# Two fused transformer blocks on one core: the mixers' turns held to a distance in TensorE's queue, and some weight splits queued behind a branch

## The chip, the cores and the metric

The kernel runs on one core of a Trainium2 chip. The metric is the device time of one execution in microseconds (us), taken as the median of several runs. Besides the runs there is one profiled execution, whose trace gives the rows below. Of the core's engines TensorE (PE) does the matmuls and its weight loads (PEld), VectorE (DVE), ScalarE (ACT) and GpSimd (POOL) do the rest, and SyncE (SP) issues most of the transfers (DMA).

## The reference

A sequence of T = 512 tokens with D = 1024 features goes through two blocks, all in fp32.

```python
# first block, two layers
for l in range(2):
    p = h @ w_in[l]                       # 1024 -> the columns of four mixers
    ya = hgrn2(pa); yb = gla(pb)          # chunked gated linear attention, chunks of 64
    yc, v_first = rwkv7(pc)               # a recurrence over the tokens, 4 heads of 64
    yd = retnet(pd)                       # chunked retention
    h = layer_norm(a * h + concat(ya, yb, yc, yd) @ w_out[l])
    f = swiglu(h) if l == 0 else moe(h)   # 2816 hidden; or 8 experts of 1408, top 2
    h = layer_norm(a * h + f)
# second block
x = x + 0.5 * rms_norm(swiglu(rms_norm(x)))                  # ffn1, 2816 hidden
x = x + rms_norm(hybrid_mixer(rms_norm(x)))                  # RG-LRU and window attention
x = x + 0.5 * rms_norm(swiglu(rms_norm(x)))                  # ffn2
```

## The kernel before

**Matmuls and weights.** Activations lie with features on the 128 partitions and the 512 tokens along the free axis. An fp32 product is made from two reduced-precision halves of each side: a value is split into hi (a copy by ScalarE, L353) and lo (a subtraction by VectorE, L354), and a block of 128 x 128 weights costs three matmuls of 512 columns: hi x hi, hi x lo, lo x hi (`mm3`, L384 to L386; in `head_steps`, which begins a stage, L444, L445 and L447). Weights are split on the chip. A `Stream` (from L643) loads them in units of eight blocks (512 KB, on SyncE's queue, into a ring of raw tiles) and cuts each unit into four pieces of 256 columns (`piece`, L673), a split each; the halves lie in a ring of ten slots, `whi` and `wlo`, and a slot is free once TensorE has used it.

**The order of the work.** The program is written as one sequence. A scheduler then gives each engine its own queue: an instruction is put there when it is ready by the scheduler's reckoning, so an engine's queue can differ from the order in the code. Two means bind it: `keep_in_program_order` pins an instruction to its place among the pinned ones, and `tc.issue_after(i)` makes what is issued inside it stand behind instruction i in the queue of i's engine (an order of issue alone, with no wait for its end).

**The weave.** The mixers of the first block (`mixer1`, L1520, once for each layer) are written as generators that yield now and then with a cost; the code between two yields is called a turn here. `weave` (L795) draws turns from three streams, always from the one whose virtual time is lowest, and adds the turn's cost over the stream's weight. The first stream is the RWKV-7 recurrence in two pairs of heads (`rwkv_pair`, L1025), with many matmuls of 16 or 32 columns on 32 x 32 or 64 x 32 tiles (L1106, L1153); the second is the projections, the `gemm` turns: long runs of 512-column matmuls into a bank of `bkA` (L384 to L386), or 256-column ones (L871 to L873); the third is HGRN2, GLA and retention (`hg`, L1326, small matmuls at L1373; `ret`, L1470). The norms of heads in the scans go through `head_rstd` (L919): a matmul (L925), a copy on ScalarE, a transpose (L929), two VectorE instructions, a root on ScalarE (L937, with a load of its function table), and four transposes back (L940), all in one turn. The hybrid mixer of the second block uses the same `weave` with five streams (L2271).

**The branch.** In the second layer the experts run one after another. Near the end of the last one stands a branch (`tc.If`, L1961) for experts that got more tokens than fit; every engine passes it, and in the trace no instruction of the overflow code runs. Ahead of it the last expert's outputs are scaled into `last` (L1981 on ScalarE, L1982 on VectorE), and the scheduler has put splits of the first pieces of the next stage's weights (`f1gu`, the second block's ffn1, L2250 and on) there as well. Behind it `combine` (L2001) adds the experts' rows to the residual: for each of eight half tiles a few matmuls (L2011, L2020, L2022), an add on VectorE (L2024) and a square on ScalarE (L2025), both pinned. Then TensorE runs ten matmuls that compute nothing needed (`warm`, L328), transposes the rows (L1988), and ffn1 starts at L444.

Of the kernel before, what the change touches and what calls it, by code (L numbers as in the profile page):

```python
# [2 lines left out]

# [1 line left out]

# [7 lines left out]
AF = mybir.ActivationFunctionType  # L13
OP = mybir.AluOpType
# [628 lines left out]
class Stream:  # L643


    def __init__(self, K_, src, pool=None, bufs=None, own=0):
        self.K, self.src, self.u, self.j, self.ahead, self.ready = K_, src, -1, 8, [], []
        self.pool, self.bufs, self.own, self.units = pool, bufs, own, 0

    def fetch(self):  # L650
        self.ahead.append(self.load())
# [21 lines left out]
    def piece(self, raw):  # L673
        k = self.K
        if self.pool and self.units > self.own:
            t = self.pool.tile([P, 2, WC], F32R, name="wx", tag="wx", bufs=self.bufs)
            hi, lo = t[:, 0], t[:, 1]
        else:
            hi = k.ws.tile([P, WC], F32R, name="whi", tag="whi", bufs=WB)
            lo = k.ws.tile([P, WC], F32R, name="wlo", tag="wlo", bufs=WB)  # L680
        k.split(raw, hi, lo)
        return hi, lo

    def block(self):
# [49 lines left out]
WEAVEA = (1.0, 1.4, 1.8)  # L734
WEAVEB = (1.0, 1.3, 1.8)
NH32 = 4
WARM = 10
AHEAD = 1
STEP, LAG, LEAD = 4, 12, 4
RINGD, RINGO = 10, 8  # L740
LAG1, LEAD1, LAG2 = 12, 2, 18
# [50 lines left out]
        return self.pool.tile(shape, dt, name=name, tag=self.tag, bufs=self.bufs)  # L792


def weave(streams, weights):  # L795


    at = [0.0] * len(streams)
    live = set(range(len(streams)))
    now = 0.0  # L800
    while live:
        for n in sorted(live, key=lambda i: at[i]):
            try:
                c = next(streams[n])
            except StopIteration:
                live.remove(n)
                break
            if c is not None:
                now = at[n]
                at[n] += c / weights[n]  # L810
                break
            at[n] = max(at[n], now)
# [707 lines left out]
def mixer1(k, l, begin):  # L1520
    tc = k.tc
    with tc.tile_pool(name="mxc", bufs=1, reuse_waits="tile") as cp, \
            tc.tile_pool(name="mxa", bufs=1, reuse_waits="tile") as ap, \
            tc.tile_pool(name="mxb", bufs=1, reuse_waits="tile") as bp:
        sl = Slots(ap, "a", NA)
        st = k.stream(f"win{l}")
        if begin:
            k.load_x(sl, st)
        m = Mix(k, l, st, cp, ap, bp)
        if begin:  # L1530
            trig(k, sl)

        def chain(*gens):
            for g in gens:
                yield from g

        weave([chain(m.rwkv_pair(0), m.rwkv_pair(1)),
               chain(m.rwkv_in((6, 2, 0, 4, 5)), m.hg_in(0), m.rwkv_in((7, 8, 3, 1)), m.hg_gate(0), m.hg_in(1),
                     m.hg_gate(1), m.ret_in()),
               chain(m.hg(0), m.hg(1), m.ret())], (WEAVEA, WEAVEB)[l])  # L1540
        sT = []
        for f in range(0, KT, 2):
            t = m.a2(("ZR", "MB")[f // 4], [P, 2, T])
            sT += [t[:, 0], t[:, 1]]
        st = k.ln_stats(sl, 1 if l else 2)[l:]
        ws = k.stream(f"wout{l}", *(() if l else (Slots(bp, "b", NB), 0, KT - 2)))
        tot = Totals(*st)
        ys = (lambda q: m.yH[q]), (lambda q: m.yL[q])
        ro = k.moe if l else None
        if ro:  # L1550
            flat = lambda t: t.rearrange("p a b c -> p (a b c)")
            ro.open(sl, *[Cut(flat(m.a2("ZL", [P, NT, 2, P]))) for _ in range(2)])
        for f in range(KT):
            k.resid_in(f, sT)
            if f >= st[0].last and not l:
                continue
            ps = k.gemm_fm(ws, ys, KT, tot.first if f == KT - 1 else None)
            k.resid_out(f, ps, sT, st)
            if ro:
                ro.logits(f, sT[f])  # L1560
        if ro:
            ro.route(sT, tot, ap, m.yH[0])
        else:
            k.ln_end(ws, ys, KT, 2 * KT, sT, k.par(f"ln1g{l}"), k.par(f"ln1b{l}"), sl, st)
        if "y" in k.dbgs:
            for f in range(KT):
                t = sl.tile([P, T])
                k.nc.vector.tensor_tensor(t, m.yH[f].bitcast(F32), m.yL[f].bitcast(F32), op=OP.add)
                k.nc.sync.dma_start(k.dbgs["y"][f], t)
# [26 lines left out]
class Moe:  # L1596
# [404 lines left out]
    def combine(self, cp, acc):  # L2001

        k, nc = self.k, self.k.nc
        V, mm, pin = nc.vector, nc.tensor.matmul, self.k.tc.keep_in_program_order
        st = [k.sm.tile([P, 8], F32, name="cst") for _ in range(NT)]
        half = lambda i, n: acc[:, i, n * 512:(n + 1) * 512]

        banks = {}
        def first(i, n):
            b = banks[i, n] = k.bankA() if n else k.bankB()  # L2010
            return mm(b, cp[:, 1, 1, 0, i * P:(i + 1) * P], cp[:, 0, n, 0], start=True, stop=False)  # L2011

        def add(i):
            sl = slice(i * P, (i + 1) * P)
            for n in range(2):
                if n:
                    first(i, n)
                b = banks[i, n]
                rs = slice(64 * n, 64 * n + 64)
                mm(b, cp[:, 1, 1, 0, sl], cp[:, 0, n, 1], start=False, stop=False)  # L2020
                for q in range(2):
                    mm(b, cp[rs, 1, 1, 1, sl], cp[rs, 1, 0, q], start=False, stop=q == 1)  # L2022
                a = half(i, n)
                pin(V.scalar_tensor_tensor(a, b, 1.0, a, op0=OP.mult, op1=OP.add, accum_out=st[i][:, n:n + 1]))  # L2024
                pin(nc.scalar.activation(b, a, AF.Square, accum_out=st[i][:, 2 + n:3 + n]))  # L2025

        def var(i):
            s = [st[i][:, c:c + 1] for c in range(8)]
            pin(V.tensor_scalar(s[4], s[0], s[1], 1.0 / D, op0=OP.add, op1=OP.mult))
            pin(V.tensor_scalar(s[5], s[2], s[3], 1.0 / D, op0=OP.add, op1=OP.mult))  # L2030
            pin(V.scalar_tensor_tensor(s[5], s[4], s[4], s[5], op0=OP.mult, op1=OP.subtract))
            pin(nc.scalar.activation(s[6], s[5], AF.Sqrt, bias=k.eps[1e-5], scale=-1.0))

        def norm(i):
            s = [st[i][:, c:c + 1] for c in range(8)]
            pin(V.reciprocal(s[6], s[6]))
            pin(V.tensor_scalar(s[7], s[4], s[6], -1.0, op0=OP.mult, op1=OP.mult))

        def scale(i):
            s = [st[i][:, c:c + 1] for c in range(8)]  # L2040
            if i == 0:
                pin(nc.gpsimd.tensor_scalar(acc[:, i], acc[:, i], s[6], s[7], op0=OP.mult, op1=OP.add))
            elif i == 1:
                pin(nc.scalar.activation(acc[:, i], acc[:, i], AF.Identity, bias=s[7], scale=s[6]))
            else:
                pin(nc.scalar.activation(half(i, 0), half(i, 0), AF.Identity, bias=s[7], scale=s[6]))
                pin(V.tensor_scalar(half(i, 1), half(i, 1), s[6], s[7], op0=OP.mult, op1=OP.add))

        for i in range(NT):
            first(i, 0)  # L2050

        nc.scalar.activation(k.sm.tile([P, 1], F32, name="root"), cp[:, 0, 1, 1, :1].bitcast(F32), AF.Sqrt, bias=k.eps[1e-5], scale=0.0)
        for i in range(NT + 2):
            if i < NT:
                add(i)
            if i == NT - 1:
                k.warm(cp[:, 1, 1, 0], WARMC, k.bankA)
            if i >= 2:
                norm(i - 2)
            if 1 <= i <= NT:  # L2060
                var(i - 1)
            if i >= 2:
                scale(i - 2)
# [105 lines left out]
class Second:  # L2169
# [73 lines left out]
    def ffn(self, n, post, nxt):  # L2243
        k, nc, tc = self.k, self.k.nc, self.k.tc
        V = nc.vector
        with tc.tile_pool(name="ffn", bufs=1) as p, tc.tile_pool(name="ffnt", bufs=2) as p2:
            hH = p.tile([P, NH, T], F32R, name="hH")
            hL = p.tile([P, NH, T], F32R, name="hL")
            Rs = self.scale_rows(p2)
            st = k.stream(f"f{n}gu")  # L2250
            xs = k.xs()
            ps = finish(k.head_steps(st, xs, 0 if n == 1 else LEAD))
            ps += [k.gemm_fm(st, xs, KT, bank=k.bankB) for _ in range(AHEAD)]
# [12 lines left out]
    def mixer(self):  # L2266
        k, tc = self.k, self.k.tc
        with tc.tile_pool(name="m2y", bufs=1) as big:
            with tc.tile_pool(name="m2", bufs=1, reuse_waits="tile") as pool:
                m = Hybrid(k, self, big, pool)  # L2270
                weave([m.project(), m.lru(), m.heads(0), m.heads(1), m.attend()], WEAVE2)  # L2271
            with tc.tile_pool(name="m2o", bufs=1) as p:
                ws = k.stream("wo2", p, RINGO, KT - 2)
                self.post(ws, ((lambda a: m.yH[a]), (lambda a: m.yL[a])), KT, 2, 2 * KT, "mpost", 1.0, "pre2", p, LEAD)
# [289 lines left out]
```

## Time and profile before

| | us |
|---|---|
| median of 3 runs | 2657.43 |
| lowest and highest | 2655.86 and 2659.28 |
| the profiled execution | 2657.86 |
| its span in the trace | 2656.1 |
| TensorE busy | 2590.3 (98%) |
| VectorE busy | 1628.9 (61%) |
| ScalarE busy | 1344.3 (51%) |
| mean granted clock of TensorE | 0.988 |

The span is what the trace covers; the execution's own time is 1.8 us more. Busy is the time in which an engine has an instruction under way. An idle time is put down to what ended it: an engine with a tile and a line, a DMA, or "issue", which means that the engine waited for nothing that the profile shows. Matmuls overlap, so a matmul's duration is longer than its distance to the next; a line with x and a number joins that many alike. The granted clock is TensorE's as a share of full speed; it has two levels, 1.2 and 2.4 GHz. "ACTq" and "DVEq" are an engine's sequencer, not its work.

### The profile page before, as it was taken

To read this page: it belongs to the slowest core of one execution; us is meant where nothing else is said; L and a number is where in the kernel's file an instruction comes from. 1 tells how busy PE (TensorE), PEld (TensorE's weight loads), DVE (VectorE), ACT (ScalarE), POOL (GpSimd) and SP (SyncE) were. 2 spreads that over 40 slices of the span, in tenths; PEclk is the share of its full clock that TensorE was granted. 3 is DMA by queue.
4 is the path that set the end of the run, shared out by engine and by line. 5 is a ranking of instruction groups with operands and counts; after the bars stand their busy time and mean duration, and the time that the engine had idled before them with its cause. 6 is when DMAs were issued, how large, how long until landed. Compare 5 with 4: busy or idle time off the path is not lost. (4 is left out here: it accounts for less than half of the span.)

```text
span 2656.1 us, 48326 instructions
## 1 busy us (share of the span) xinstructions
PE 2590.3 (98%) x18669; PEld 2115.0 (80%) x18669; DVE 1628.9 (61%) x3383; ACT 1344.3 (51%) x2789; POOL 308.6 (12%) x391
## 2 busy tenths in 40 slices
PE   8999999999999999999999999999999999999998
PEld 6777688888877676798888888688888877888887
DVE  6655565444466555467888888665553578655533
ACT  5465344333343554366666666554433467444432
POOL 1101120000030010042233233100000100100000
PEclk9999999999999999999999999899999999999999
DMA  4111413223321112279887878523222212132222
GB/s 161 46 53 50 158 66 110 95 96 97 110 81 43 56 50 72 73 231 340 276 274 265 283 278 262 179 81 101 96 96 95 90 56 87 65 102 97 95 96 72
DMA packets 96330, 334.39 MB, mean 126 GB/s; under 512 B 12079, under 2 KB 15631, under 8 KB 96096
## 3 DMA queue, kind: packets, MB, share of 16 engines
q1 hardware_dynamic: 87520, 305.61, 34.3%
q0 software_dynamic: 8000, 24.95, 3.0%
q8 instruction: 149, 2.44, 0.4%
q10 hardware_dynamic: 576, 0.69, 0.1%
q14 instruction: 85, 0.70, 0.1%
HBM read 313.76 MB, written 17.45 MB: 125 GB/s over the span
## 5 line engine op out<-in xcount | busy, mean ns | idle before, releaser
L353 ACT ACTIVATE whi<-wraw 128x256 fp32r<-128x256 f32 x1172 | 475.9, 415 | 773.9 <-PE bkA L385 712.2
L354 DVE TENSOR_TENSOR wlo<-wraw,whi 128x256 fp32r<-128x256 f32 x1172 | 486.7, 423 | 582.6 <-ACT whi L353 563.2
L384 PE MATMUL bkA<-xH,whi 128*128 128x512 f32 x1352 | 537.2, 397 | 2.1 <-DVE sh L964 1.8
L385 PE MATMUL bkA<-xL,whi 128*128 128x512 f32 x1352 | 535.8, 396 | 0.0
L386 PE MATMUL bkA<-xH,wlo 128*128 128x512 f32 x1352 | 531.7, 393 | 0.0
L1921 PE MATMUL bkA<-xe,mhi 128*128 128x320 f32 x1392 | 358.3, 344 | 3.0 <-POOL xe L1782 1.6
L384 PEld LDWEIGHTS bkA<-xH,whi 128*128 128x128 f32 x1352 | 254.2, 188 | 68.7 <-issue 13.6
L385 PEld LDWEIGHTS bkA<-xL,whi 128*128 128x128 f32 x1352 | 254.6, 188 | 58.3 <-issue 9.6
L386 PEld LDWEIGHTS bkA<-xH,wlo 128*128 128x128 f32 x1352 | 254.2, 188 | 58.6 <-issue 7.0
L1923 PE MATMUL bkA<-xe,mlo 128*128 128x160 f32 x1218 | 287.7, 236 | 1.2 <-DVE mlo L354 1.2
L1921 PEld LDWEIGHTS bkA<-xe,mhi 128*128 128x128 f32 x1392 | 250.1, 189 | 4.3 <-POOL xe L1782 2.4
L1923 PEld LDWEIGHTS bkA<-xe,mlo 128*128 128x128 f32 x1218 | 233.1, 191 | 1.8 <-DVE mlo L354 1.7
L384 PE MATMUL bkA<-hH,whi 128*128 128x512 f32 (+1 forms) x548 | 204.2, 373 | 0.0
L385 PE MATMUL bkA<-hL,whi 128*128 128x512 f32 (+1 forms) x548 | 203.9, 372 | 0.0
L386 PE MATMUL bkA<-hH,wlo 128*128 128x512 f32 (+1 forms) x548 | 203.7, 372 | 0.0
L354 DVE TENSOR_TENSOR mlo<-mraw,mhi 128x1024 fp32r<-128x1024 f32 x105 | 139.9, 1334 | 36.8 <-ACT mhi L353 33.9
L353 ACT ACTIVATE mhi<-mraw 128x1024 fp32r<-128x1024 f32 x105 | 110.4, 1054 | 24.4 <-PE bkA L2096 11.1
L354 DVE TENSOR_TENSOR mlo<-wraw,mhi 128x1024 fp32r<-128x1024 f32 x79 | 104.6, 1327 | 23.1 <-ACT mhi L353 21.5
L385 PEld LDWEIGHTS bkA<-hL,whi 128*128 128x128 f32 x548 | 103.2, 188 | 18.1
L384 PEld LDWEIGHTS bkA<-hH,whi 128*128 128x128 f32 x548 | 103.2, 188 | 17.9
L386 PEld LDWEIGHTS bkA<-hH,wlo 128*128 128x128 f32 x548 | 103.1, 188 | 17.8
L354 DVE TENSOR_TENSOR mlo<-mlow,mhi 128x1024 fp32r<-128x1024 f32 x78 | 105.8, 1358 | 18.5 <-ACT mhi L353 15.9
(738 smaller groups left out, 4424.2 us busy)
## 6 DMA issues: line engine op xcount, KB each, us to landing
mraw<-moew SPq DMA_DIRECT2D x105, 512.0 KB
wraw<-moew SPq DMA_DIRECT2D x81, 512.0 KB
mlow<-moew SPq DMA_DIRECT2D x78, 512.0 KB
wraw<-win SPq DMA_DIRECT2D x76, 512.0 KB
wraw<-f0gu SPq DMA_DIRECT2D x44, 512.0 KB
wraw<-f1gu SPq DMA_DIRECT2D x44, 512.0 KB
wraw<-f2gu SPq DMA_DIRECT2D x44, 512.0 KB
wraw<-f0d SPq DMA_DIRECT2D x22, 512.0 KB
```

The lines of the kernel that those rows point to most:

```text
L353: nc.scalar.activation(hi, x, AF.Copy)
L354: nc.vector.tensor_tensor(lo, x, hi.bitcast(F32), op=OP.subtract)
L384: mm(ps, wH, xH, start=first, stop=False)
L385: mm(ps, wH, xL, start=False, stop=False)
L386: mm(ps, wL, xH, start=False, stop=last)
L1921: mm(ps, wH, xf[:, q], start=q == 0, stop=last, skip_group_check=True)
L1923: mm(ps[:, :C], wL, xe[:, q, 0], start=False, stop=False, skip_group_check=True)
```

## The change

`weave` gets the tile context and a distance, `behind`. It notes the last TensorE instruction of each turn that has any, and issues each turn inside `tc.issue_after` of the one noted `behind` turns ago. `mixer1` passes `BEHIND = 12`; the hybrid mixer passes a number that is never reached. The second part: `combine` notes its first add and its first square in `k.hold`; ffn1's stream takes this as `st.hold`, and the splits of its first two units (eight pieces) are issued inside `tc.issue_after` of these two. Both are orders of issue; no instruction is added, and none leaves.

```diff
 class Stream:
     def __init__(self, K_, src, pool=None, bufs=None, own=0):
-        self.pool, self.bufs, self.own, self.units = pool, bufs, own, 0
+        self.pool, self.bufs, self.own, self.units, self.hold = pool, bufs, own, 0, None
...
     def piece(self, raw):
...
-        k.split(raw, hi, lo)
+        with ExitStack() as order:
+            if self.hold and self.units <= 2:
+                for i in self.hold:
+                    order.enter_context(k.tc.issue_after(i.ins))
+            k.split(raw, hi, lo)
         return hi, lo
...
+BEHIND = 12
...
-def weave(streams, weights):
+def weave(tc, streams, weights, behind):
+    traced = tc.nc.cur_bb.bb.instructions
+    ends = []
+
+    def turn(s):
+        n = len(traced)
+        with tc.issue_after(ends[-behind]) if len(ends) >= behind else nullcontext():
+            c = next(s)
+        new = [i for i in traced[n:] if i.engine == mybir.EngineType.PE]
+        if new:
+            ends.append(new[-1])
+        return c
...
-                c = next(streams[n])
+                c = turn(streams[n])
...
 def mixer1(k, l, begin):
...
-        weave([chain(m.rwkv_pair(0), m.rwkv_pair(1)),
+        weave(tc, [chain(m.rwkv_pair(0), m.rwkv_pair(1)),
...
-               chain(m.hg(0), m.hg(1), m.ret())], (WEAVEA, WEAVEB)[l])
+               chain(m.hg(0), m.hg(1), m.ret())], (WEAVEA, WEAVEB)[l], BEHIND)
...
     def combine(self, cp, acc):
...
+        k.hold = None
...
-                pin(V.scalar_tensor_tensor(a, b, 1.0, a, op0=OP.mult, op1=OP.add, accum_out=st[i][:, n:n + 1]))
-                pin(nc.scalar.activation(b, a, AF.Square, accum_out=st[i][:, 2 + n:3 + n]))
+                done = (pin(V.scalar_tensor_tensor(a, b, 1.0, a, op0=OP.mult, op1=OP.add, accum_out=st[i][:, n:n + 1])),
+                        pin(nc.scalar.activation(b, a, AF.Square, accum_out=st[i][:, 2 + n:3 + n])))
+                k.hold = k.hold or done
...
     def ffn(self, n, post, nxt):
...
             st = k.stream(f"f{n}gu")
+            if n == 1:
+                st.hold = k.hold
...
     def mixer(self):
...
-                weave([m.project(), m.lru(), m.heads(0), m.heads(1), m.attend()], WEAVE2)
+                weave(tc, [m.project(), m.lru(), m.heads(0), m.heads(1), m.attend()], WEAVE2, 10 ** 6)
```

## Rows read from the trace of the kernel before

**Rows 1.** The page's part 1: busy us (share of the span) and instructions.

```profile
PE 2590.3 (98%) x18669; PEld 2115.0 (80%) x18669; DVE 1628.9 (61%) x3383; ACT 1344.3 (51%) x2789; POOL 308.6 (12%) x391
```

**Rows 2.** Table by stage: window, us, busy by engine, PEclk, DMA share, GB/s.

```profile
7.00:337.00 330.00, 319.17 (x4046) 235.33 (x4047) 196.72 (x494) 173.37 (x346) 29.77 (x53) 0.98 0.27 90
...
745.00:1082.00 337.00, 321.79 (x4108) 237.21 (x4109) 204.15 (x504) 170.48 (x342) 43.43 (x66) 0.98 0.19 62
...
1703.00:1735.00 32.00, 29.29 (x88) 16.80 (x89) 16.78 (x49) 17.08 (x36) 1.20 (x1) 0.68 0.06 18
```

**Rows 3.** TensorE's waits, 30:330: line, what ended them, us, times, longest us.

```profile
PE bkB L1373 <- issue: 2.6, 2, 1.9
PE bkB L1153 <- issue: 2.5, 3, 1.8
...
PE bkB L1106 <- issue: 0.5, 1, 0.5
```

**Rows 4.** TensorE's waits, 770 to 1010 us.

```profile
PE bkB L1153 <- issue: 5.0, 3, 2.1
PE bkB L1373 <- DVE Qp L1348: 1.4, 1, 1.4
...
PE bkA L871 <- issue: 0.8, 1, 0.8
PE bkB L1106 <- issue: 0.8, 1, 0.8
```

**Rows 5.** Table by stretches of 10 us, columns as in rows 2.

```profile
60.00:70.00 10.00, 9.83 (x274) 7.64 (x275) 2.64 (x7) 3.32 (x7) 0.00 (x0) 0.83 0.05 7
190.00:200.00 10.00, 9.45 (x227) 8.75 (x227) 4.56 (x10) 6.56 (x8) 0.00 (x0) 0.66 0.01 3
```

**Rows 6.** TensorE's timeline from 56 us: start, us, line, tiles, count, [idle before].

```profile
60.17 0.44 PE L1153 MATMUL bkB<-XT,Y 32*32 32x16 f32 x33 [1.75 <-issue]
...
61.25 0.78 PE L384 MATMUL bkA<-xH,whi 128*128 128x512 f32 x1
```

**Rows 7.** Timeline of TensorE, from 40 us.

```profile
46.21 0.39 PE L384 MATMUL bkA<-xH,whi 128*128 128x512 f32 x1
46.55 0.66 PE L940 MATMUL bkB<-ca,kk 128*128 128x128 f32 x4
```

**Rows 8.** Timelines of ScalarE, VectorE and TensorE at the branch.

```profile
1700.78 1.34 ACT L353 ACTIVATE whi<-wraw 128x256 fp32r<-128x256 f32 x4 [2.29 <-DMA wraw<-f1gu]
...
1703.39 0.41 DVE L354 TENSOR_TENSOR wlo<-wraw,whi 128x256 fp32r<-128x256 f32 x1
1703.72 0.74 DVE L1982 SCALAR_TENSOR_TENSOR last<-bkA,gs,last 128x512 fp32r<-128x512 f32 x1
1704.39 0.41 DVE L354 TENSOR_TENSOR wlo<-wraw,whi 128x256 fp32r<-128x256 f32 x1
...
1703.97 0.50 PE L2011 MATMUL bkB<-last 128*128 128x512 f32 x1 [1.41 <-ACTq L1961]
1705.19 1.08 PE L2011 MATMUL bkB<-last 128*128 128x512 f32 x3 [0.71 <-DVEq L1961]
```

**Rows 9.** Six stretches together, matmuls into bkA alone: length, busy time.

```profile
sum 16.50, PE 16.37; mean PE 2.73
```

**Rows 10.** Timeline of ScalarE, from 44 us.

```profile
44.57 1.28 ACT L937 ACT_TABLE_LOAD   x1
45.86 0.63 ACT L937 ACTIVATE kk<-hr 128x512 f32<-128x512 f32 x1
```

**Rows 11.** Timeline of TensorE, from 946 us.

```profile
950.33 0.76 PE L1373 MATMUL bkB<-Qp,KX 64*32 64x32 f32 x64 [1.43 <-DVE Qp L1348]
```

**Rows 12.** Timelines of VectorE and TensorE in the combine and behind it.

```profile
1710.19 0.69 DVE L2024 SCALAR_TENSOR_TENSOR x<-bkA,x 128x512 f32<-128x512 f32 x1 [1.60 <-PE bkA L2022]
...
1722.60 4.29 PE L328 MATMUL bkA<-last 128*128 128x512 f32 x10
...
1731.41 0.50 PE L444 MATMUL bkA<-xH,whi 128*128 128x512 f32 x1 [1.02 <-DVE x L1997]
```

More of the change, by code (lines that the diff above doesn't have):

```diff
@@ L1 @@
 import math
-from contextlib import ExitStack
+from contextlib import ExitStack, nullcontext
 import numpy as np
```

## The prediction

> **What bounds the kernel now.** I read the page's busy times first: TensorE is busy 98% of the span, VectorE 61%, ScalarE 51% [rows 1], so only what TensorE waits for, or does slowly, can pay. The table by stage then says where that is. In the first mixer's weave (7 to 337 us) TensorE is idle 330.00 - 319.17 = 10.8 us and its mean granted clock is 0.98; in the second's (745 to 1082 us) it is idle 337.00 - 321.79 = 15.2 us, again at 0.98; in the 32 us around the branch the clock is 0.68 [rows 2]. All that the change touches lies in these three stages, some 700 of 2656 us.
>
> Inside the weaves two kinds of loss stand out. First, the waits of TensorE: those that end with "issue" (nothing that the profile shows) come to 2.6 + 2.5 + 0.5 us in the first weave [rows 3] and 5.0 + 0.8 + 0.8 us in the second [rows 4], 12.2 us in all, nearly all at L1153, L1373 and L1106, the lines with the small matmuls. Waits for another engine are less: the longest is 1.4 us, for VectorE's Qp [rows 4]. Second, the clock: seven stretches of 10 us have a granted clock under 1.00, six of them 0.83 and one 0.66 (the first and the 0.66 one are shown) [rows 5]. A share of 0.83 means that a third of the stretch was at 1.2 instead of 2.4 GHz. Work that TensorE does at half speed takes twice as long, so the clock costs at most 6 x 1.7 + 3.4 = 13.6 us.
>
> One place shows both: a run of small matmuls stops for 1.75 us for "issue", goes on at 60.17, and the gemm matmul at 61.25 takes 0.78 us [rows 6], against 0.39 for one at 46.21 [rows 7].
>
> **The change, part by part.**
>
> *Holding the turns.* Nothing is computed differently: no matmul, split or load is added. What is held is the order of TensorE's queue alone. A turn of the weave that runs more than twelve TensorE turns ahead may not be issued before the older one is; in practice these are gemm turns of the projection stream, which are always ready and fill the waits of the scans. A held gemm turn takes its matmuls with it and, since it gives its weight tiles back later, the splits of later units on ScalarE and VectorE and the loads behind them on SyncE's queue come later too, by the same few microseconds; nothing else is queued there that TensorE waits for, and the DMA share in these stages is 0.27 and 0.19 [rows 2], so I cost that at nothing. If that cover were gone a unit of eight blocks would be late once, and ScalarE's wait for such a load is 2.29 us where the trace has one [rows 8].
>
> What it can cost. A norm of the scans (`head_rstd`) is one turn with two round trips inside; while it runs, TensorE does gemm turns. One such hop runs matmul after matmul up to 46.21, then come the norm's transposes at 46.55 [rows 7]. If these gemm turns are held behind the norm's own last transposes, the hop stays open. Counting the turns in the code's order, the gemm turns in six of the hops are more than twelve turns ahead. The gemm work in the held part of the six hops sums to 16.4 us [rows 9]; this is the upper bound of this cost, and nothing is the lower (the turns could be placed elsewhere, or arrive with less lead). I take 58% of it: in a hop that lasts 3.3 us, the table load (1.28 us) and the root (0.63 us) on ScalarE [rows 10] are 1.91 us that cannot shrink, and the rest, which includes splits of the very gemm turns, can. That is +9.5 us.
>
> What it can bring. The turns that are held come back later, and the later places are the runs of small matmuls, where TensorE now stalls for "issue" and then runs at half clock. The ceiling is 12.2 + 13.6 = 25.8 us; the floor is nothing, or below it, if the opened hops cost clock in their turn (a rival below). I take 60%: in four of the seven slow stretches the gemm turns stand directly ahead of the small matmuls, as ahead of 950.33, where the projections have run through and TensorE then waits 1.43 us for VectorE before its 64 small matmuls [rows 11]. That is -15.5 us.
>
> The weak point is the "issue" waits of up to 2.1 us [rows 4]: no row names what releases them. I take it that small matmuls packed close together bring them on, so that gemm turns set between would hide them. If they belong to places in TensorE's instruction stream, whatever turn stands there, they move but stay; that is the first rival. The Trainium skill, "Runtime: NRT & Kernel Launch", section "Instruction fetch mechanics", leans to that side: an engine's sequencer fetches instructions by itself in blocks of fixed size, ahead of need, so that what a crossing costs ("mostly hidden") hangs on the count of instructions and not on their order.
>
> *The splits behind the branch.* Eight ScalarE splits and eight VectorE splits of the next stage's first two units leave the place ahead of the branch and stand behind the first add of the combine. Now TensorE has done its last matmul of the experts and waits 1.41 us until ScalarE, and again 0.71 us until VectorE, is past the branch [rows 8]. VectorE's last two pieces of work ahead of the branch are a needed one (1703.72, 0.74 us) and a split (1704.39, 0.41 us); a second split (1703.39) stands between two needed ones [rows 8]. If all splits leave, VectorE is done 0.8 us sooner; if the pieces of the third unit, which the change does not hold, stay, only about 0.25 us. I take -0.6. The splits then fall into VectorE's idle 1.60 us before each add [rows 12]; if that cover were gone, eight of 0.41 us would add up to 3.3 us, the upper bound. They are needed when the next stage's matmuls start at 1731.41 [rows 12], and the loads that they release on SyncE's queue serve only units after these. If a shorter wait kept the clock up, the ten warming matmuls of 4.29 us [rows 12] would take half, and the combine less; that is the lower end, -10 us, and I do not count on it.
>
> *The other weave* is given a distance that no turn reaches: nothing.
>
> **Sum.** +9.5 - 15.5 - 0.6 = -6.6 us. The profiled execution took 2657.86 us (span 2656.1), 0.4 above the median of the three runs, 2657.43. 2657.9 - 6.6 = 2651.3; I give 2651.
>
> **Rivals.**
>
> *The two effects cancel, or the order barely changes.* For it: TensorE is 97 and 95% busy in the weaves [rows 2], few turns run far ahead, and if the "issue" waits don't depend on the order of the turns the first ceiling falls away. Against it: each weave has three hops that must open. The weaves then give 9.5 - 0.6 x 13.6 = +1.3 us, and the whole 2657.9 + 1.3 - 0.6 = 2658.6; chance 0.26.
>
> *Slower: the opened hops.* The six hops of [rows 9] open in full width (16.4 us), and TensorE, idle for most of 3 us where it now never stops, loses its clock after each: six times 1.7 us as in [rows 5], 10.2 us. It decides once the opened hops cost over 16.1 us, what the gains above give. For it: these hops are now filled to the last tenth, the gemm turns are needed anyway, and the projection stream still has work long after the scans of the first pair, so filling a hop now loses nothing later. Against it: the trace's slow stretches follow small matmuls, with TensorE 9.83 us of 10 busy in the first of them [rows 5], and not idle time. The Trainium skill, "TensorE: Matmul & The Clock Gate", section "HAM oscillation — how this bites in real kernels", has it the other way: pauses between bursts of matmuls are what brings the array back to half clock. With the hops at 9.5 us, the clock at 10.2 and 4 us of the stalls saved it gives 2657.9 + 15.7 = 2673.6; chance 0.30.
>
> *The branch alone*: if the turns kept their order, 2657.9 - 0.6 = 2657; this counts with the 0.26.
>
> **How the numbers follow.** The forecast has 0.44. Its own range is 2637 (all of the ceiling, with 5 us of hops) to 2652.5. To leave no more than 2 in 10 out, the range goes on through the second case to 2676, just past the third's value. A measurement of this kernel tells about 0.2% (5.3 us) from no change. So faster 0.44, same 0.26, slower 0.30; the likeliest case alone is faster by a quarter of a percent, close to that line.
>
> **What would show it.** Right: in the weaves the "issue" waits at L1153 and L1373 fall to about half, fewer than seven stretches have a clock under 1.00, and the idle time of TensorE in the six hops rises by about 10 us. At the branch the first combine matmul after VectorE's arrival starts 0.3 to 0.8 us sooner and no split of the first two units stands ahead of it. Wrong: idle of 3 us at each norm with no fewer "issue" waits, or new stretches at half clock behind the norms; or unchanged rows at 43 to 47 us, which would mean that the order did not move.

## The result, and the profile after

The changed kernel takes 2679.26 us (median of 4 runs, 2675.97 to 2680.48), the kernel before 2658.36 in the same comparison: a ratio of 1.0078, 95% interval 1.0058 to 1.0099. It is slower by 20.9 us. The profiled execution took 2680.31 us, its span is 2678.6, 22.5 more than the span of before.

The page's part 1 shows nothing of it: TensorE is busy 3 us longer than in [rows 1], all else is the same to a few us.

```profile
PE 2593.3 (97%) x18669; PEld 2119.6 (79%) x18669; DVE 1629.6 (61%) x3383; ACT 1343.8 (50%) x2789; POOL 305.7 (11%) x391
```

Where the time went is read off by putting the two traces side by side at the same matmul, counted from the start (both have 18669). The first weave takes 343.6 us instead of 329.8, the second 351.8 instead of 336.0, the stage of the router behind it 179.9 instead of 177.9; the experts 442.9 instead of 444.0; the combine (first matmul behind the branch to the first of ffn1) 19.5 instead of 27.4. From there to the end the distance stays at 22.4 us, the hybrid mixer's weave included. So the weaves lost 29.6 us, and the branch gave 7.9 back.

The table by stage of the changed kernel, for the two weaves and the combine (columns as in [rows 2]):

```profile
7.40:351.10 343.70, 323.85 (x4048) 238.99 (x4048) 195.66 (x494) 173.58 (x345) 29.21 (x53) 0.96 0.26 86
759.70:1111.50 351.80, 327.10 (x4104) 240.28 (x4104) 205.38 (x502) 168.95 (x340) 39.54 (x64) 0.96 0.19 59
1734.30:1753.80 19.50, 17.39 (x74) 10.22 (x74) 14.33 (x53) 16.12 (x39) 1.47 (x1) 1.00 0.16 55
```

In the weaves TensorE is idle 343.70 - 323.85 = 19.9 and 351.80 - 327.10 = 24.7 us, 44.5 in all; before it was 25.6 in the same stretches. The granted clock is 0.96 in both, where [rows 2] has 0.98. Added up from the trace's records of the clock, 54.6 us of the two weaves were at half clock, before 27.3. Half of the difference, 13.7 us, is what the clock can have cost, and 18.9 us is the idle time; together 32.6, for the 29.6 measured. In the combine the clock is 1.00, where the 32 us of [rows 2] have 0.68.

TensorE's waits in the first weave (7 to 351 us), then in the second (759 to 1111.4 us), columns as in [rows 3]. Left out at the top is the wait for the very first weights, 6.9 us here and 7.0 before:

```profile
...
PE bkB L1390 <- DVE Qp L1365: 4.2, 1, 4.2
PE bkB L957 <- ACT kk L954: 3.4, 2, 1.9
PE bkB L1390 <- issue: 3.4, 2, 2.0
PE bkB L1402 <- DVE KX L1375: 1.4, 1, 1.4
PE bkB L1170 <- issue: 1.3, 1, 1.3
...
PE bkB L957 <- ACT hr L954: 0.6, 1, 0.6
```

```profile
PE bkB L1170 <- DVE X L1163: 4.5, 1, 4.5
PE bkB L1170 <- issue: 3.5, 2, 2.4
PE bkB L1390 <- DVE KX L1375: 3.1, 3, 1.7
PE bkB L1390 <- DVE Qp L1365: 3.1, 1, 3.1
...
PE bkB L957 <- ACT kk L954: 0.9, 1, 0.9
PE bkB L957 <- ACT hr L954: 0.6, 1, 0.6
```

These answer to [rows 3, 4]. L957 are the transposes of a norm (L940 before), L1390 and L1170 the scans' small matmuls (L1373 and L1153 before). The waits for "issue" come to 3.4 + 1.3 + 3.5 = 8.2 us. New are the waits for VectorE: 4.2 and 3.1 us for Qp, 4.5 for X, where the longest was 1.4. Added up over all lines of both weaves, TensorE's waits for VectorE come to 24.3 us instead of 7.5, those for ScalarE to 11.1 instead of 4.9. The norms' transposes, on which the prediction hung its cost, account for 3.4 + 0.6 + 0.9 + 0.6 = 5.5 us.

What stands in such a wait is seen in the timeline. Before, between two steps of the second pair's scan:

```profile
911.49 1.10 PE L1093 MATMUL bkB<-ZR,kk 64*64 64x128 f32 x32
912.52 0.50 PE L386 MATMUL bkA<-xH,wlo 128*128 128x512 f32 x1
...
915.87 0.39 PE L385 MATMUL bkA<-xL,whi 128*128 128x512 f32 x1
916.76 0.72 PE L1153 MATMUL bkB<-X,LbT 32*32 32x16 f32 x64 [0.51 <-DVE X L1146]
```

and the same two steps after:

```profile
933.09 1.10 PE L1110 MATMUL bkB<-ZR,kk 64*64 64x128 f32 x32 [0.94 <-DVE kk L1087]
938.70 1.05 PE L1170 MATMUL bkB<-X,LbT 32*32 32x16 f32 x64 [4.51 <-DVE X L1163]
```

Before, gemm matmuls run from 912.52 until 915.87 (15 of them, cut here to the first and the last), while VectorE prepares X. After, TensorE stands for 4.51 us: by the rule of the change the next gemm turn stands behind a turn twelve back that is itself not issued yet. The held turns were what filled this wait; and since the idle time of the weaves rose by 18.9 us, they did not pay elsewhere what they cost here. They come later: behind the recurrence's last small matmul the first weave now has 20 more matmuls into bkA than before, the second 35 more.

### The profile page after: what moved, and what is told of

The parts are those of the page before. It is cut to its first block, busy times and chain, and to the rows that moved or that the text cites. A ratio compares the mean times of both kernels' runs of the same rounds, so it can differ in the third digit from the quotient of the medians.

```text
span 2678.6 us, 48323 instructions
## 1 busy us (share of the span) xinstructions
PE 2593.3 (97%) x18669; PEld 2119.6 (79%) x18669; DVE 1629.6 (61%) x3383; ACT 1343.8 (50%) x2789; POOL 305.7 (11%) x391
## 5 line engine op out<-in xcount | busy, mean ns | idle before, releaser
L384 PE MATMUL bkA<-xH,whi 128*128 128x512 f32 x1352 | 544.2, 403 | 2.3 <-DVE sh L981 1.9
```

Source lines behind the costliest of these rows:

```text
L384: mm(ps, wH, xH, start=first, stop=False)
```

## The experiments

In all of them the columns are read at the same matmuls as above. "Held" is the distance of the turns, "behind" says whether the splits are queued behind the combine's first add. Idle and half clock are sums over both weaves. The stretch at the branch goes from the last expert matmul to the first of ffn1.

| kernel | held | splits behind | weave 1, 2 (us) | idle | half clock | branch | median of runs |
|---|---|---|---|---|---|---|---|
| before | no | no | 329.8, 336.0 | 25.6 | 27.3 | 29.2 | 2658.4 (4) |
| e7, before again | no | no | 330.4, 337.6 | 24.1 | 34.1 | 29.1 | 2656.4 (1) |
| the change | 12 | yes | 343.6, 351.8 | 44.5 | 54.6 | 20.7 | 2679.3 (4) |
| e1 | 12 | no | 335.1, 351.5 | 42.6 | 44.4 | 20.8 | 2676.4 (4) |
| e2 | no | yes | 329.8, 335.4 | 23.2 | 30.8 | 20.7 | 2651.7 (10) |
| e3 | 24 | yes | 328.9, 339.3 | 25.3 | 30.8 | 20.7 | 2657.1 (10) |
| e4 | 12, from first | yes | 343.1, 349.7 | 41.9 | 61.4 | 20.7 | 2677.6 (4) |
| e5 | 6 | no | 354.6, 375.5 | 64.6 | 78.5 | 20.8 | 2724.4 (2) |
| e6 | 18 | no | 334.7, 344.8 | 29.6 | 51.2 | 29.2 | 2667.2 (8) |
| e8 | no | yes, 3 units | 328.8, 334.1 | 24.3 | 23.9 | 20.7 | 2649.6 (10) |
| e9 | 12, not gemm | yes | 332.2, 339.5 | 30.9 | 27.3 | 20.7 | 2651.8 (10) |
| e10 | no | no, pause filled | 329.5, 337.5 | 24.3 | 34.2 | 21.1 | 2652.4 (10) |
| e11 | no | yes, pause longer | 329.4, 337.1 | 29.3 | 20.5 | 30.6 | 2663.3 (10) |

The kernel before ran beside them 63 times: 2644 to 2669 us, medians 2656.0 (beside e1 to e4), 2656.4 (e5 to e8) and 2657.0 (e9 to e11). One and the same program differs by 25 us from execution to execution; 8.5 us of this turned out to arise at the branch (e7, e10, e11), the rest is not explained. So the one traced execution of a kernel need not be a typical one: e1's took 2667.2 us, the fastest of its four, those of e6 (2673.7) and e9 (2657.0) are the slowest of theirs. The ratios below are to the kernel before that ran beside, with the 95% interval in brackets.

**The two parts alone.** e1 keeps the hold of the turns and drops that of the splits; e2 keeps that of the splits and gives the turns a distance that is never reached. Their edits to the changed kernel:

```diff
-                st.hold = k.hold
+                st.hold = None
```

```diff
-BEHIND = 12
+BEHIND = 10 ** 6
```

> Only the hold of the turns; the splits of ffn1 stay where the kernel before has them. Theory A (the hold costs both weaves some 30 us, the branch earns some 9 by itself): about 2658 + 31 = 2689 us, the stretch from the last expert matmul to the first ffn1 matmul again 29 us long. Rival B (the branch got faster because everything ahead of it had moved, not because of the splits): about 2680 us, that stretch 21 us long.

> Only the splits behind the branch; the turns are given a distance that is never reached. Theory A: both weaves as before (330 and 336 us), the stretch at the branch about 21 us instead of 29, the time about 2658 - 9 = 2649 us. Rival B: the branch is as slow as before, about 2657 us.

e2: 2651.7 us, ratio 0.999 (0.9971 to 1.0009), weaves as before, 20.7 us at the branch, as theory A had it. e1: 2676.4 us, ratio 1.0094 (1.0057 to 1.0131). The cost is the hold of the turns. But e1's stretch at the branch is 20.8 us, not 29, though its splits stand ahead of the branch. Here are its combine and TensorE's two waits there, first the table by stage, then the timeline:

```profile
1720.10:1739.20 19.10, 17.14 (x74) 10.28 (x74) 12.04 (x42) 12.47 (x28) 1.20 (x1) 1.00 0.07 27
```

```profile
1720.15 0.50 PE L2029 MATMUL bkB<-last 128*128 128x512 f32 x1 [1.32 <-ACTq L1978]
1721.36 0.96 PE L2029 MATMUL bkB<-last 128*128 128x512 f32 x3 [0.71 <-DVEq L1978]
```

The waits, 1.32 and 0.71 us, are nearly those of [rows 8], 1.41 and 0.71, and yet the clock stayed at 1.00. So neither theory was right about the branch: the splits' place doesn't decide it, and rival B's shift doesn't explain e2 against before. A third one was needed.

**The distance of the turns.** e3, e6 and e5 set the distance to 24, 18 and 6; e6 and e5 drop the hold of the splits as e1 does.

```diff
-BEHIND = 12
+BEHIND = 24
```

> The whole change with a distance of 24 turns instead of 12; in the order of before no turn leads by more than about 32. Theory A1 (what costs is each gemm turn that is taken out of a wait of the scans, so the cost follows their number): the weaves cost under 8 us, about 2650 to 2657 us. Rival C (any bound on the order upsets the scheduler's placing and costs much the same): near the change, 2670 us or more.

> The hold of the turns alone, with a distance of 6 instead of 12. Theory A1 (each held gemm turn is one that filled a wait of the scans): TensorE's idle time in the two weaves, 25.6 us in the kernel before and 42.6 us with twelve turns alone, rises further, to 55 us or more, and the time to 2690 us or more. Rival E (the cost comes from a few particular places that twelve already opens): idle within 5 us of 42.6, the time about 2677 us. At the branch the splits stand as in the kernel before: if they decide the clock there, the stretch is 27 us long; if the clock falls there in some executions only, either 19 or 27.

> The hold of the turns alone, with a distance of 18. Theory A1: idle in the weaves between that of 24 turns (25.3 us) and that of 12 (42.6), about 28 to 36 us, the time about 2660 to 2668 us. Rival E: as with 12 or as with 24, nothing between. The branch as for the run with 6.

TensorE's idle time in the weaves goes 25.3, 29.6, 42.6 to 44.5, 64.6 us for 24, 18, 12 and 6, and the medians 2657.1, 2667.2, 2676.4 to 2679.3, 2724.4 us. Rivals C and E are out: the cost grows step by step as the distance shrinks, as A1 would have it (the held turns themselves were not counted). The idle time alone does not show the step to 18, for e11 below, which holds no turn, has 29.3 us; the time shows it, and a wait of 3.1 us for Qp that stands in e6's second weave as with 12, while the one of 4.5 us for X does not. e3 reads 1.0011 (0.9988 to 1.0033), e6 1.0042 (1.0018 to 1.0065), e5 1.0254 (1.0191 to 1.0317). But e3 holds the splits as well, so its partner is e2 and not the kernel before: its median is 5.4 us above that of e2, with runs that overlap. With 6 the weaves read (columns as in [rows 2]):

```profile
7.40:362.00 354.60, 328.43 (x4047) 239.41 (x4047) 197.01 (x493) 172.56 (x343) 28.65 (x53) 0.95 0.25 83
770.30:1145.80 375.50, 337.08 (x4104) 244.71 (x4105) 204.28 (x502) 171.21 (x340) 39.22 (x64) 0.94 0.17 55
```

Idle is 26.2 and 38.4 us, the clock 0.95 and 0.94. What opens between 12 and 6 are the norms. TensorE's waits at their transposes with 6, in the first weave and then in the second:

```profile
PE bkB L957 <- ACT kk L954: 5.3, 2, 3.0
PE bkB L957 <- ACT hr L954: 4.9, 3, 2.0
...
PE bkB L957 <- ACT gn L954: 0.6, 1, 0.6
```

```profile
PE bkB L957 <- ACT hr L954: 6.7, 4, 2.0
PE bkB L957 <- ACT kk L954: 6.1, 2, 3.0
...
PE bkB L957 <- ACT gn L954: 2.4, 2, 1.8
```

That is 26.0 us against 5.5 in e1, 20.5 of the 22.0 us by which the idle time grew; the waits for VectorE, 25.3 us in all, are hardly more than e1's 24.2.

**Which held turns cost.** e4 holds a turn behind the first TensorE instruction of the older turn instead of its last; e9 never holds the projection stream.

```diff
-            ends.append(new[-1])
+            ends.append(new[0])
```

```diff
-        with tc.issue_after(ends[-behind]) if len(ends) >= behind else nullcontext():
+        with tc.issue_after(ends[-behind]) if len(ends) >= behind and s is not streams[1] else nullcontext():
```

> The whole change, but a turn is held behind the first TensorE instruction of the turn twelve back instead of its last, so a norm's turn no longer bars gemm turns until its last transposes. Rival D (the opened hops of the norms, where a turn ends late, are the cost): the waits at the norm's transposes go and with them the clock lost behind them, about 2650 to 2660 us. Theory A1 (gemm turns are missing all through the scans, above all where VectorE is awaited and in the runs of small matmuls): only the 5.5 us of waits at these transposes can go, about 2670 to 2677 us.

> The whole change with twelve turns, but turns of the projection stream (the gemm turns) are never held; those of the two scan streams are. Theory A1: the held gemm turns are all of the cost, so TensorE's idle time in the weaves is 23 to 26 us and the time that of the version with the splits alone, about 2650 us. Rival F (a bound on the scans' own turns costs too): idle over 30 us, 2660 us or more.

e4 takes 2677.6 us, 1.0097 (1.006 to 1.0135). Of its waits in the first weave the largest in the scans and the one left at the norms' transposes:

```profile
PE bkB L1170 <- DVE X L1163: 4.1, 2, 3.7
...
PE bkB L1390 <- DVE Qp L1365: 2.1, 1, 2.1
...
PE bkB L957 <- ACT hr L954: 0.7, 1, 0.7
```

The norms' hops are closed but for 0.7 us there, and 0.6 and 0.2 in the second weave, and the time is what it was. Rival D, which was also the mechanism of the prediction's slower rival, is out for a distance of twelve. e9, with the gemm turns free and all others held, takes 2651.8 us, 0.998 (0.9959 to 1.0000), the same as e2. Its idle time, 30.9 us, missed the forecast of 23 to 26; but e11, where nothing is held, has 29.3, so programs with free gemm turns scatter from 23.2 to 29.3 and e9 lies close above. What is more in e9 are the waits for "issue", 16.6 us; those for VectorE are 8.2 us as in e2. At the step where TensorE stood for 4.51 us in the changed kernel, e9 has the 15 gemm matmuls again, and the wait is short (e1 and e4 have none of them there and wait 4.5 us):

```profile
920.21 0.72 PE L1170 MATMUL bkB<-X,LbT 32*32 32x16 f32 x64 [0.48 <-DVE X L1163]
```

In time the hold of the scans' own turns costs nothing that shows.

**The branch.** e7 is the kernel before without any edit; e8 is e2 with one unit more held:

```diff
-            if self.hold and self.units <= 2:
+            if self.hold and self.units <= 3:
```

> The kernel before, once more, for a second trace. If what the clock does differs from execution to execution of the same program: TensorE's idle time in the weaves is again 25 to 26 us, while the stretches at half clock lie elsewhere or add up to another sum than 68.2 us, the branch among them (19 or 27 us). If the program fixes them: the same stretches within a few tenths of a us, 27 us at the branch.

> Only the splits, with the third unit's pieces held as well. Theory of the branch as a matter of chance: the stretch at the branch is 19 to 20 us whatever is held, and the time is that of the two-unit version, 2648 to 2655 us. If the splits ahead of the branch still delay it: VectorE passes the branch up to 0.4 us sooner and the time is that much lower. Loss: if the splits then come late for ffn1's first matmuls, TensorE waits at its start for a wlo, 1 us or more.

e7 has the branch again at 29.1 us, and elsewhere a different clock from the first trace of the same program: 20.5 us at half in the second weave instead of 13.7. Of the five traces with the splits ahead of the branch, three (before, e7, e6) have the combine at half clock and two (e1, e5) don't, with the same two waits of TensorE in all. Of the six with the splits behind it and nothing else done to the pause (the change, e2, e3, e4, e8, e9) none has. There the waits are shorter; in the changed kernel:

```profile
1734.32 0.50 PE L2029 MATMUL bkB<-last 128*128 128x512 f32 x1 [0.82 <-DVE last L1999]
1735.19 0.96 PE L2029 MATMUL bkB<-last 128*128 128x512 f32 x3 [0.37 <-DVEq L1978]
```

0.82 and 0.37 us instead of 1.41 and 0.71. Theory P, that this pause is what lets the clock fall, and only sometimes, was then tried from both sides. Neither holds turns. e10 leaves the splits ahead of the branch and fills the first wait; its code of the branch is moved behind the experts' last matmuls, where the queues have it anyway, and the needless matmuls go to a bank taken early. e11 leaves the splits behind it and lengthens the wait.

```diff
...
+                if e + 1 == NE:
+                    b = at[1]
+                    with tc.issue_after(end.ins):
+                        for _ in range(12):
+                            end = mm(b[:, :2 * P], hid[:, 0, 0], hid[:, 0].rearrange("p a c -> p (a c)"), start=True, stop=True)
+                    with tc.If(counts[0] > LIM, label="overflow"):
...
```

```diff
...
+            nc.scalar.activation(hi, yb[1], AF.Copy, scale=gs[0])
+            V.scalar_tensor_tensor(lo, yb[1], gs[0], hi.bitcast(F32), op0=OP.mult, op1=OP.subtract)
         self.combine(cp, acc)
```

> The kernel before (no turn held, splits ahead of the branch), with twelve needless matmuls of 256 columns behind the last expert matmul, still ahead of the branch, in the 1.3 to 1.4 us that TensorE waits there for ScalarE. Theory P (the pause ahead of the combine lets the clock fall in some executions, and then the combine takes 27 us instead of 19): filled, it never falls there; 19 to 20 us in the trace, and the runs lie as low and as close together as with the splits held, about 2650 us, none above 2658. Theory S (the splits themselves, ahead of the branch, are the cost): as the kernel before, 2656 us with single runs up to 2666.

> The splits held, no turn held, but ScalarE and VectorE do their last scaling ahead of the branch twice, so that TensorE's pause there is again as long as in the kernel before (about 2.0 us and more instead of 1.2). Theory P: the clock falls there in some executions again; the runs scatter over some 20 us like those of the kernel before and their median is 4 us or more above the 2650 of the splits alone, of which 0.7 to 1.3 us is the doubled work itself. Theory S: the splits are behind the branch, so the median is 2651 to 2653 us and no run is above 2660.

e10's timeline of TensorE, then e11's, then e11's combine in the table by stage:

```profile
1700.60 1.60 PE L1990 MATMUL bkB<-hid 128*128 128x256 f32 x12
1703.40 1.17 PE L2034 MATMUL bkB<-last 128*128 128x512 f32 x4 [1.20 <-DVEq L1991]
```

```profile
1705.93 0.50 PE L2031 MATMUL bkB<-last 128*128 128x512 f32 x1 [2.33 <-ACTq L1978]
1706.80 0.96 PE L2031 MATMUL bkB<-last 128*128 128x512 f32 x3 [0.37 <-DVEq L1978]
```

```profile
1705.90:1733.80 27.90, 25.81 (x75) 14.55 (x75) 14.58 (x52) 16.38 (x39) 1.47 (x1) 0.63 0.12 39
```

e10: 2652.4 us, all ten runs between 2647.6 and 2655.2, 0.9985 (0.9965 to 1.0005); the branch takes 21.1 us. e11: 2663.3 us, all ten between 2657.7 and 2665.4, 1.002 (1.0001 to 1.004); the clock is 0.63 in the combine, and the branch takes 30.6 us. Theory P's forecasts hold in both, S's in neither. For e10 the medians alone do not say it, since the interval includes 1, nor does one trace at full clock where two of five had it anyway; what does is that none of its ten runs is above 2655.3, while 13 of the 25 of the kernel before beside it are. Nor is the pause gone in e10: 1.20 us are left of it, as much as the 0.82 and 0.37 us of the changed kernel together. Only the scatter that P forecast for e11 didn't come: no run was below 2657 us, as if the longer pause let the clock fall every time.

So the splits' place is worth 0.1 us by itself (20.8 against 20.7 us in the traces), and 8.5 us in those executions in which the clock would have fallen. All 30 runs of e2, e8 and e9 lie between 2643.1 and 2657.1, median 2651.4; of the 63 of before, median 2656.3, 26 lie above 2657.2.

**The version to keep** is that of the splits without the hold of the turns: e8, 2649.6 us, 0.997 (0.9948 to 0.9992), is the fastest of all and beats both kernels; e2 with two units can't be told from it.

## Why the prediction was wrong

It gave 2651 us, 2637 to 2676, with 0.44 for faster; the measured 2679.3 lies 3.3 above the range. The slower rival (0.30, 2673.6) had the side and nearly the size, the size in part by luck: the hops, on which it hung the loss, cost 5.5 us and not the 9.5 of its sum.

*What the hold brings (-15.5).* This step failed most. It let the held gemm turns come back in the runs of small matmuls, and mend both the "issue" waits and the clock there. They come from there: at 912 us of the kernel before they stand between the scan's small matmuls, and the hold takes them away. The clock went the other way, 27.3 us at half becoming 54.6; the three traces with twelve turns have 44.4 to 61.4, the seven with free gemm turns 20.5 to 34.2. The "issue" waits did go from 12.2 to 8.2 us. They are 7 to 8.5 us in the traces with twelve turns and 9 to 16.6 in those with free gemm turns, the kernel before in its second trace at 9.9, so a gain of some 4 us is likely, of the 15.5 in the sum. What these waits are is not shown. The Trainium skill, "Runtime: NRT & Kernel Launch", section "Instruction fetch mechanics", calls what it costs to cross from one block of instructions to the next mostly hidden. No run here shows whether these waits are such crossings.

*What it costs (+9.5).* The upper bound, 16.4 us [rows 9], was no bound. It counted the gemm work in six hops of the norms alone. The hops cost 5.5 us, but waits of the scans for VectorE that were filled open too, 24.3 us instead of 7.5; the idle time rose by 18.9 us. e4 closes the hops and keeps the price. At a distance of six the hops do open, for 26.0 us. The prediction had a row that could have shown it: 1.43 us of waiting ahead of 950.33, at a place where the gemm turns ahead were used up [rows 11], which it read as a surplus of gemm turns ahead and not as a want of them there.

*The slower rival.* Its place (the hops) is refuted by e4 for the distance of twelve, its second half is not: TensorE, idle where it never stopped, loses its clock. The Trainium skill, "TensorE: Matmul & The Clock Gate", section "HAM oscillation — how this bites in real kernels", has pauses between bursts of matmuls as what brings the array back to half clock. At the branch the runs agree: filled, the pause left the clock at 1.00, lengthened, 0.63. The prediction set against it that slow stretches follow small matmuls in a TensorE busy 9.83 us of 10 [rows 5]. That is so too, and how much of the weaves' half clock goes with the pauses and how much with the bare runs of small matmuls was not tried apart.

*The splits (-0.6).* Direct effect: 0.1 us. TensorE's waits ahead of the combine got 0.9 us shorter, as the step said, and 0.6 came back at ffn1's first matmul, which waits 1.64 us for VectorE instead of 1.02 [rows 12]. The splits do fall into VectorE's idle time, and no wlo is late. The lower end, -10 us if the shorter wait kept the clock, which it did not count on, is close to what the two profiled executions show, 29.2 and 20.7 us at the branch.

*The base.* The sum was set against one profiled execution. Its 20.5 us at half clock in the combine are a matter of that execution; with a program that scatters over 25 us no single trace carries a term of 8.5.

*Right*: the other weave, at no distance, gave nothing; splits, loads and DMA in the weaves (DMA share 0.26 and 0.19) cost nothing.

## What to carry to other kernels

Before bounding how far independent work may run ahead, list every wait that this work fills, on each engine and in each stream, and not only the longest hops; what a bound takes out of a wait is lost unless another wait of the same length lies ahead. Keep TensorE's pause short at a join that all engines pass, and put work that isn't needed yet behind the join: a pause of 2 us can cost 8.5 us of clock behind it. Take more than one trace before costing a clock loss, for the same program may show it in one execution and not in the next.

## What was not expected of the hardware

The granted clock is no property of the program. The same combine, after the same two waits of TensorE (1.3 to 1.4 and 0.71 us), ran at half clock for 20.5 us in three traces and at full clock in two; after waits of 0.82 and 0.37 us it never fell in six traces, after 2.33 and 0.37 us it fell in the one trace taken, and no run of that kernel was below 2657 us. Once it had fallen it stayed down for 20.5 us, through the matmuls of the combine and most of the ten that compute nothing needed, although TensorE has no wait in that time: of the 27.90 - 25.81 = 2.1 us that it is idle in e11's stretch, 0.37 lie ahead of the fall and 1.69 at the very end, when the clock was back at full; in the weaves the stretches at half clock ended after 3.4 to 17 us. The weaves scatter too: e1's first weave, the same program as the change's, took 335.1 us instead of 343.6, with 13.7 us at half clock instead of 27.3.
